# Scores on two halves of TensorE's rows, and units of the dilated attention taken two at a time

## The chip, the cores and the metric

One core of a Trainium2 chip runs the whole kernel. It has TensorE (matmuls, into PSUM), VectorE, ScalarE and GpSimd (called POOL in the profile), and SyncE, whose queue issues most of the transfers. The metric is the time of one execution on the device in microseconds; the median of several is given. Lower is better.

## The reference

The reference is a trunk of two layers on 512 tokens of width 1024, in float32. Each layer is a norm, a mixer, a residual, a norm, a gated feed-forward part with a short convolution, a residual. The mixer of layer 0 is a gated DeltaNet beside a dilated window attention (8 heads of 64); that of layer 1 is a retention (4 heads, keys of 64, values of 128) beside a Hyena convolution. The change touches the two parts that multiply q with k. The dilated attention is, cut to what matters:

```python
q, k = rope(q), rope(k)                      # 8 heads, 64 wide
for window, dilation in ((128, 1), (512, 4), (2048, 16)):
    s = where(valid, q @ k.T * 64 ** -0.5, -1e30)      # banded, per residue class of the dilation
    o_p, lse_p = softmax(s) @ v, logsumexp(s)
o = sum_p softmax_p(lse_p) * o_p
```

The retention is, for both directions together, `o = ((q @ k.T) * decay) @ v` per head, where decay depends on the distance of two tokens, followed by a norm and a gate; q and k are rotated here too.

## The kernel before

Everything is one program on one core, written with tiles; a planner orders the instructions of each engine, mostly in the order in which the program gives them, and takes a later one first where an earlier one is not ready by its own estimate of times. PSUM is two pools of four banks: `acc` and `wk`. A matrix product in float32 is done as three fp32r matmuls on a split of each operand into hi and lo (`mm3`, lines 263 to 265). Weights come by SyncE's queue in 512 KB pieces, and ScalarE and VectorE split them (lines 251 and 252).

The dilated attention (`dilated`) joins its three patterns into one softmax over all 512 keys, with the logarithm of the number of patterns that allow a distance added to the score (`lnc`). Two heads of 64 lie in one tile of 128 rows, a pair p. Its q and k come from a projection (`proj_t`), and are rotated: `rope_in` copies PSUM to SBUF and swaps halves by four DMAs; `rope_out` multiplies, adds, and makes the matmul operands. For q it makes for each head a tile of 128 rows that has hi in one half of the rows and lo in the other; for k (`moving`) one with hi in both halves, by a copy on POOL, and one with lo in one half and zeros in the other. So a score tile of a head, `mm_stack`, is two matmuls over 128 rows: (hi + lo) of q with hi of k, and hi of q with lo of k.

The work goes in 16 units (p, i): pair p, block i of 128 queries. `scores` makes for each of the two heads a 128 x 512 score tile in a `wk` bank; VectorE adds lnc, takes the extreme and writes smx (line 524), ScalarE takes the exponential with its sum (line 525), VectorE the reciprocal, POOL scales (line 529). `turn` transposes the two tiles on TensorE into `acc` banks (line 535), and ScalarE and VectorE copy one each into pT (line 537). `pv` multiplies with v: each matmul is 128 rows by 64 columns, the two heads of the pair on two halves of the columns (line 546). In the loop over u the scores are those of unit u, the transposes those of u - 2, the products those of u - 3; at u = 0, 2, 5 and 8 the projection of a later q or k stands behind them, at u = 10 and 18 a piece of the gates of the next part (`tail`).

The retention (`retention`) has two pairs s of two heads. For each head h, `scores(h)` makes four score tiles by `mm_stack` in `wk` banks, and VectorE multiplies each with the decay `gen` into sd (line 1079); the decays of all four heads are made ahead. Then 16 matmuls in plain float32 (two passes each) multiply with v (line 1089). The scores of head h + 1 are put ahead of the products of head h. Before this, `proj_tok` makes v: four pieces of weights, 24 matmuls for each, into four `acc` banks, which ScalarE copies out (line 1060).

Of the kernel before, what the change touches and what calls it, by code (L numbers as in the profile page):

```python
# [162 lines left out]
class K:  # L163
# [129 lines left out]
    def proj_tok(self, n, out_fn, filler=None):  # L293

        accs = [self.acc(nm=f"pt{t}") for t in range(NT)]
        for c in range(4):
            w = self.get()
# [163 lines left out]
    def rope_out(self, pool, rope, t, sw, moving, tag, bufs):  # L461


        nc = self.nc
        nc.gpsimd.tensor_mul(sw, sw, rope[:, 1, :])
        nc.vector.tensor_mul(t, t, rope[:, 0, :])
        nc.vector.tensor_add(t, t, sw)
        o = pool.tile([128, 4 if moving else 2, S], F32R, tag=tag, name=tag, bufs=bufs)
        half = [slice(0, 64), slice(64, 128)]
        for e in range(2):  # L470
            a, b = half[e], half[1 - e]
            nc.scalar.copy(o[a, e], t[a])
            nc.vector.tensor_sub(o[a, 2 + e] if moving else o[b, e], t[a], o[a, e])
            if moving:
                nc.gpsimd.memset(o[b, 2 + e].bitcast(F32), 0.0)
                nc.gpsimd.tensor_copy(o[b, e], o[a, e])
        return o
# [5 lines left out]
    def mm_stack(self, out, a, b, e, cols):  # L483
        self.nc.tensor.matmul(out, a[:, e, cols], b[:, e], start=True, stop=False)
        self.nc.tensor.matmul(out, a[:, e, cols], b[:, 2 + e], start=False, stop=True)
# [14 lines left out]
    def dilated(self, n, tail):  # L500
        nc, I = self.nc, self.I
        V = nc.vector
        with ExitStack() as ctx:
# [7 lines left out]
            def project(p, what, ps=None):  # L511
# [3 lines left out]
                qk[p, what] = self.rope_out(dp, rope, *self.rope_in(dp, ps)[:2], what == "k", "d" + what, 3)  # L515
# [40 lines left out]
            for i in range(4):  # L556
# [3 lines left out]
                if i < 2:  # L560
                    qk[0, "qk"[i]] = self.rope_out(dp, rope, *rin[i][:2], i == 1, "d" + "qk"[i], 3)
            with self.tc.issue_after(rin[3][2].ins):
                for i in (2, 3):
                    qk[1, "qk"[i % 2]] = self.rope_out(dp, rope, *rin[i][:2], i == 3, "d" + "qk"[i % 2], 3)
# [841 lines left out]
```

## Time and profile before

| | |
|---|---|
| median of 3 runs | 1319.92 us (1319.66 to 1320.06) |
| the profiled execution | 1319.69 us, of which the profile's span is 1317.9 us |
| TensorE busy | 1302.9 us, 6977 matmul records |
| VectorE, ScalarE, POOL busy | 750.7, 526.9, 144.4 us |
| dilated attention, scores to last product | from 61 to 135 us |
| retention, scores and products | from 748.7 to about 770 us |

How to read it: a matmul's recorded duration includes the time until its last result is written, so matmuls overlap in the record; what one costs TensorE is its pitch, from its start to the start of the next. "L484" is line 484. A float32 matmul that isn't fp32r is recorded as two passes. In a timeline, neighbours of one line are merged into one row with a count, from the first start to the last end.

### The profile page before, as it was taken

Reading aid. Unit: us, or ns where it says so; the run is one execution under the profiler, and the core shown is the slowest. Engines: PE = TensorE matmul, PEld = TensorE weight load, DVE = VectorE, ACT = ScalarE, POOL = GpSimd, SP = SyncE. Lnnn points to the kernel's source line nnn. Section 1 sums busy time; section 2 is a strip of 40 time slices with the busy share of each in tenths; the row PEclk is TensorE's granted clock in tenths of the full one; section 3 lists DMA queues with packets and bytes.
Section 4 is the critical chain, followed back from the end, with each engine's and each line's share of the span. In section 5 each row is a group of like instructions: output and inputs, shape, how many; then the busy total and the mean of one; then the engine's idle time right before and its main releaser. Section 6 shows DMA issues by size and latency. Waiting matters only on the chain.

```text
span 1317.9 us, 17629 instructions
## 1 busy us (share of the span) xinstructions
PE 1302.9 (99%) x6977; PEld 1092.6 (83%) x6977; DVE 750.7 (57%) x1089; ACT 526.9 (40%) x837; POOL 144.4 (11%) x175
## 2 busy tenths in 40 slices
PE   8999999999999999999999999999999999999997
PEld 7877888888988888888889887888888888888886
DVE  5777659977744432444437828879754443344432
ACT  5466548235433321333326334532433331133332
POOL 2454120013000000000002200024100000000001
PEclk9999999999999999999999999999999999999999
DMA  7430113411333332333323513330343333233321
GB/s 227 127 103 25 52 33 112 130 49 61 119 101 99 98 96 81 112 96 96 96 80 112 163 41 100 93 96 19 90 122 99 99 99 96 81 113 96 96 80 64
DMA packets 161025, 123.61 MB, mean 94 GB/s; under 512 B 6985, under 2 KB 134477, under 8 KB 160944
## 3 DMA queue, kind: packets, MB, share of 16 engines
q1 hardware_dynamic: 160798, 122.43, 31.6%
q8 instruction: 55, 0.90, 0.3%
q14 instruction: 26, 0.21, 0.1%
q10 hardware_dynamic: 146, 0.07, 0.0%
HBM read 117.23 MB, written 2.10 MB: 91 GB/s over the span
## 4 chain that ended last, share of the span: by engine, by line
PE 87%; DVE 7%; ACT 2%; DMA 1%; issue 1%; SPq 1%; POOL 1%; POOLq 0%; ACTq 0%; DVEq 0%
PE gup L264 11%; PE gup L265 11%; PE gup L263 11%; PE oacc L264 7%; PE oacc L265 7%; PE oacc L263 7%; PE pt L263 2%; PE pt L264 2%; PE pt L265 2%; PE first L264 2%; PE first L265 2%; PE first L263 2%; PE ap L263 1%; PE ap L264 1%; PE ap L265 1%; PE hap L263 1%
## 5 line engine op out<-in xcount | busy, mean ns | idle before, releaser
L252 DVE TENSOR_TENSOR wlo<-raw,whi 128x1024 fp32r<-128x1024 f32 x192 | 236.2, 1232 | 305.0 <-ACT whi L251 300.3
L251 ACT CAST whi<-raw 128x1024 fp32r<-128x1024 f32 (+1 forms) x197 | 206.1, 1047 | 424.7 <-PE gup L264 183.7
L263 PE MATMUL gup<-hh,whi 128*128 128x512 f32 x656 | 255.2, 389 | 0.0
L264 PE MATMUL gup<-hl,whi 128*128 128x512 f32 x656 | 255.2, 389 | 0.0
L265 PE MATMUL gup<-hh,wlo 128*128 128x512 f32 x656 | 255.2, 389 | 0.0
L263 PEld LDWEIGHTS gup<-hh,whi 128*128 128x128 f32 x656 | 123.2, 188 | 25.6
L264 PEld LDWEIGHTS gup<-hl,whi 128*128 128x128 f32 x656 | 123.2, 188 | 25.4
L265 PEld LDWEIGHTS gup<-hh,wlo 128*128 128x128 f32 x656 | 123.2, 188 | 25.4
L263 PE MATMUL oacc<-whi,ghi 128*128 128x512 f32 x352 | 137.1, 389 | 0.0
L265 PE MATMUL oacc<-whi,glo 128*128 128x512 f32 x352 | 137.0, 389 | 0.0
L264 PE MATMUL oacc<-wlo,ghi 128*128 128x512 f32 x352 | 136.9, 389 | 0.0
L265 PEld LDWEIGHTS oacc<-whi,glo 128*128 128x128 f32 x352 | 66.1, 188 | 13.7
L263 PEld LDWEIGHTS oacc<-whi,ghi 128*128 128x128 f32 x352 | 66.1, 188 | 13.7
L264 PEld LDWEIGHTS oacc<-wlo,ghi 128*128 128x128 f32 x352 | 66.1, 188 | 13.6
L428 DVE TENSOR_TENSOR sl<-gup,sl 128x512 f32<-128x512 f32 x42 | 29.0, 692 | 81.1 <-PE gup L265 81.1
L313 DVE TENSOR_TENSOR x<-oacc,x 128x512 f32<-128x512 f32 x64 | 43.2, 684 | 48.6 <-PE oacc L265 48.6
L427 ACT ACTIVATE sl<-c 128x512 f32<-128x512 f32 x44 | 27.8, 632 | 89.2 <-DVE c L365 89.2
L263 PE MATMUL first<-hh,whi 128*128 128x256 f32 x192 | 54.9, 288 | 0.0
L264 PE MATMUL first<-hl,whi 128*128 128x256 f32 x192 | 54.4, 284 | 0.2 <-DVE hl L224 0.2
L265 PE MATMUL first<-hh,wlo 128*128 128x256 f32 x192 | 54.2, 283 | 0.0
L104 POOL TENSOR_SCALAR ss<-ss 128x1 f32<-128x1 f32 x16 | 5.0, 311 | 429.3 <-ACT jk L102 429.3
L263 PE MATMUL pt<-whi,hh 128*128 128x512 f32 x128 | 50.1, 391 | 0.1
(422 smaller groups left out, 2336.4 us busy)
## 6 DMA issues: line engine op xcount, KB each, us to landing
raw<-in_ffn_w_in_dram SPq DMA_DIRECT2D x88, 512.0 KB, 3.8
raw<-in_ffn_w_out_dram SPq DMA_DIRECT2D x44, 512.0 KB, 3.7
raw<-in_ab_w_in_dram SPq DMA_DIRECT2D x28, 512.0 KB, 3.9
raw<-in_cd_w_in_dram SPq DMA_DIRECT2D x24, 512.0 KB, 4.6
x<-in_x_dram SPq DMA_DIRECT2D x16, 256.0 KB, 4.2
raw<-in_ab_w_out_dram SPq DMA_DIRECT2D x8, 512.0 KB
raw<-in_cd_w_out_dram SPq DMA_DIRECT2D x8, 512.0 KB, 3.6
rs<-rt SPq DMA_DIRECT2D x32, 64.0 KB, 2.0
```

Source lines behind the costliest of these rows:

```text
L104: nc.gpsimd.tensor_scalar(ss[:, 1:2], ss[:, 0:1], s, EPS, op0=ALU.add, op1=ALU.add)
L251: self.nc.scalar.copy(hi, raw)
L252: (self.nc.gpsimd if self.pool_lo else self.nc.vector).tensor_tensor(lo, raw, hi, op=ALU.subtract)
L263: mm(out, a[0], b[0], start=start, stop=False)
L264: mm(out, a[0], b[1], start=False, stop=False)
L265: return mm(out, a[1], b[0], start=False, stop=stop)
L313: self.nc.vector.tensor_add(xs, acc, xs)
L427: nc.scalar.activation(sl, c, AF.Silu)
L428: nc.vector.tensor_mul(sl, up, sl)
```

## The change

`mm_stack` is replaced by `mm_pair`: a matmul takes only the 64 rows of its head, three of them make a score tile (hi with hi, hi with lo, lo with hi), and those of the two heads of a pair alternate, the one on rows 0 to 63 and the other on rows 64 to 127, each into a bank of its own. So `rope_out` needs only hi and lo of the whole tile, by one copy on ScalarE and one subtraction on VectorE; the copies and fills on POOL go, and the tile is half as large for k. In the dilated part the loop takes two units at a time: scores of u and u + 1 (a projection directly behind the scores of its unit), transposes of u - 2, products of u - 4 and u - 3, transposes of u - 1; smx has eight buffers, not six. In the retention, `scores(s)` does both heads of a pair, with the decays of these two heads ahead of it; the first stands ahead of the last of the four pieces of v's projection (`RS` = 3), the second behind the products of the first head; sd has three buffers for each j, not two.

```diff
-    def proj_tok(self, n, out_fn, filler=None):
+    def proj_tok(self, n, out_fn, within={}):
 
         accs = [self.acc(nm=f"pt{t}") for t in range(NT)]
         for c in range(4):
+            within.get(c, lambda: None)()
...
-    def rope_out(self, pool, rope, t, sw, moving, tag, bufs):
-
+    def rope_out(self, pool, rope, t, sw, tag, bufs):
 
         nc = self.nc
         nc.gpsimd.tensor_mul(sw, sw, rope[:, 1, :])
         nc.vector.tensor_mul(t, t, rope[:, 0, :])
         nc.vector.tensor_add(t, t, sw)
-        o = pool.tile([128, 4 if moving else 2, S], F32R, tag=tag, name=tag, bufs=bufs)
-        half = [slice(0, 64), slice(64, 128)]
-        for e in range(2):
-            a, b = half[e], half[1 - e]
-            nc.scalar.copy(o[a, e], t[a])
-            nc.vector.tensor_sub(o[a, 2 + e] if moving else o[b, e], t[a], o[a, e])
-            if moving:
-                nc.gpsimd.memset(o[b, 2 + e].bitcast(F32), 0.0)
-                nc.gpsimd.tensor_copy(o[b, e], o[a, e])
+        o = pool.tile([128, 2, S], F32R, tag=tag, name=tag, bufs=bufs)
+        self.split(o[:, 0], o[:, 1], t)
         return o
 
     def rope_room(self):
 
         return self.xp.tile([128, 2, S], F32, tag="xn", name="room")
 
-    def mm_stack(self, out, a, b, e, cols):
-        self.nc.tensor.matmul(out, a[:, e, cols], b[:, e], start=True, stop=False)
-        self.nc.tensor.matmul(out, a[:, e, cols], b[:, 2 + e], start=False, stop=True)
+    def mm_pair(self, outs, a, b, cols):
+
+        for x, y in ((0, 0), (0, 1), (1, 0)):
+            for e in range(2):
+                r = slice(64 * e, 64 * e + 64)
+                self.nc.tensor.matmul(outs[e], a[r, x, cols], b[r, y], start=x + y == 0, stop=x == 1)
...
             def scores(p, i):
                 st = self.sm.tile([128, 6], F32, tag="st", name="st", bufs=8)
                 o = 384 - 128 * i
-                for e in range(2):
-                    sp = self.wk(nm="sp")
-                    self.mm_stack(sp, qk[p, "q"], qk[p, "k"], e, slice(i * 128, i * 128 + 128))
-                    s_ = dp.tile([128, S], F32, tag="smx", name="smx", bufs=6)
+                sps = [self.wk(nm="sp") for _ in range(2)]
+                self.mm_pair(sps, qk[p, "q"], qk[p, "k"], slice(i * 128, i * 128 + 128))
+                for e, sp in enumerate(sps):
+                    s_ = dp.tile([128, S], F32, tag="smx", name="smx", bufs=8)
...
-            for u in range(len(units) + 3):
-                if u < len(units):
-                    scores(*units[u])
-                if 0 <= u - 2 < len(units):
-                    turn(*units[u - 2])
-                if 0 <= u - 3:
-                    pv(*units[u - 3])
-                if later and u in DPROJ[:4]:
-                    project(*later.pop(0))
+            nu = len(units)
+            for u in range(0, nu + 4, 2):
+                for w in (u, u + 1):
+                    if w < nu:
+                        scores(*units[w])
+                    if later and w in DPROJ[:4]:
+                        project(*later.pop(0))
+                for w in (u - 2, u - 4, u - 3, u - 1):
+                    if w == u - 2 or w == u - 1:
+                        if 0 <= w < nu:
+                            turn(*units[w])
+                    elif 0 <= w:
+                        pv(*units[w])
                 if u in DPROJ[4:]:
...
-            self.proj_tok(n, lambda t, a: nc.scalar.copy(v[:, t, :], a))
...
-            def scores(h):
-                q, k = qk[0, h // 2], qk[1, h // 2]
+            def scores(s):
+                for h in (2 * s, 2 * s + 1):
+                    nc.scalar.activation(gen[:, h, :], rel[0], AF.Copy, scale=ld[:, h:h + 1])
+                    V.scalar_tensor_tensor(gen[:, h, :], rel[1], ld[:, 4 + h:5 + h], gen[:, h, :], op0=ALU.mult, op1=ALU.add)
+                    nc.scalar.activation(gen[:, h, :], gen[:, h, :], AF.Exp)
                 for j in range(4):
-                    sp = self.wk(nm="rsp")
-                    self.mm_stack(sp, k, q, h % 2, slice(j * 128, j * 128 + 128))
-                    t = rp.tile([128, S], F32, tag=f"sd{j}", name=f"sd{j}", bufs=2)
+                    sps = [self.wk(nm="rsp") for _ in range(2)]
+                    self.mm_pair(sps, qk[1, s], qk[0, s], slice(j * 128, j * 128 + 128))
                     o = 384 - 128 * j
-                    V.tensor_mul(t, sp, gen[:, h, o:o + 512])
-                    sd[h, j] = t
-
-            scores(0)
+                    for e, sp in enumerate(sps):
+                        h = 2 * s + e
+                        t = rp.tile([128, S], F32, tag=f"sd{j}", name=f"sd{j}", bufs=3)
+                        V.tensor_mul(t, sp, gen[:, h, o:o + 512])
+                        sd[h, j] = t
+
+            self.proj_tok(n, lambda t, a: nc.scalar.copy(v[:, t, :], a), {RS: lambda: scores(0)})
             O = [self.acc((128, 4, 128), f"ro{t}") for t in range(4)]
             for h in range(4):
-                if h < 3:
-                    scores(h + 1)
                 for i in range(4):
                     for j in range(4):
                         nc.tensor.matmul(O[i][:, h, :], sd[h, j][:, i * 128:(i + 1) * 128], v[:, j, h * 128:(h + 1) * 128], start=(j == 0), stop=(j == 3))
+                if h == 0:
+                    scores(1)
...
+RS = 3
```

## Rows read from the trace of the kernel before

**Rows 1.** The page: span, busy time of two engines, the chain by engine.

```profile
span 1317.9 us, 17629 instructions
...
PE 1302.9 (99%) x6977; PEld 1092.6 (83%) x6977; DVE 750.7 (57%) x1089; ACT 526.9 (40%) x837; POOL 144.4 (11%) x175
...
PE 87%; DVE 7%; ACT 2%; DMA 1%; issue 1%; SPq 1%; POOL 1%; POOLq 0%; ACTq 0%; DVEq 0%
```

**Rows 2.** Busy times by stretches: PE, PEld, DVE, ACT, POOL (instructions), clock, DMA.

```profile
91.00:105.00 14.00, 14.00 (x107) 11.42 (x107) 10.96 (x24) 9.27 (x20) 6.17 (x8) 1.00 0.22 57
115.00:130.00 15.00, 15.00 (x140) 12.30 (x140) 12.16 (x33) 10.46 (x26) 7.49 (x11) 1.00 0.01 2
```

**Rows 3.** Timeline of TensorE, one unit: start, length, line, tile, count.

```profile
93.97 0.50 PE L484 MATMUL sp<-dk,dq 128*128 128x512 f32 x1
94.31 0.40 PE L485 MATMUL sp<-dk,dq 128*128 128x512 f32 x1
...
95.02 1.03 PE L535 MATMUL tp<-ident,smx 128*128 128x128 f32 x8
95.98 1.09 PE L546 MATMUL op<-pT,dv 128*64 128x128 f32 x16
97.01 0.50 PE L484 MATMUL sp<-dk,dq 128*128 128x512 f32 x1
```

**Rows 4.** The same, cut where the shape changes (from 93.70 and from 95.75).

```profile
93.44 0.61 PE L546 MATMUL op<-pT,dv 128*64 128x128 f32 x8
...
95.56 0.49 PE L535 MATMUL tp<-ident,smx 128*128 128x128 f32 x3
```

**Rows 5.** All score matmuls of the dilated part: shortest, median, longest.

```profile
L484 PE MATMUL sp<-dk,dq x32: 387/397/504, 61.1 to 127.8; 128*128 128x512 f32 x32
...
L485 PE MATMUL sp<-dk,dq x32: 390/393/499, 61.3 to 128.0; 128*128 128x512 f32 x32
```

**Rows 6.** Timeline of TensorE, 64x64 transposes on two halves of the rows.

```profile
267.85 0.41 PE L917 MATMUL vp<-ident,P 64*64 64x64 f32 x4
...
269.35 0.63 PE L917 MATMUL vp<-ident,P 64*64 64x64 f32 x12 [0.20 <-DVE P L903]
```

**Rows 7.** All of these transposes: shortest, median, longest.

```profile
L917 PE MATMUL vp<-ident,P x32: 216/216/245, 267.8 to 272.0; 64*64 64x64 f32 x32
```

**Rows 8.** Evictions and exponentials of smx: shortest, median, longest.

```profile
L524 DVE CUSTOM_DVE_ANT_0 smx<-sp,lnc x32: 657/686/692, 61.7 to 129.3; 128x512 f32<-128x512 f32 x32
L525 ACT ACTIVATE smx<-smx,st x32: 706/722/728, 62.7 to 130.1; 128x512 f32<-128x512 f32 x32
```

**Rows 9.** Copies of the transposed tiles: shortest, median, longest.

```profile
L537 DVE COPY pT<-tp x16: 670/685/692, 72.0 to 133.4; 128x512 f32<-128x512 f32 x16
L537 ACT COPY pT<-tp x16: 562/586/587, 72.0 to 133.1; 128x512 f32<-128x512 f32 x16
```

**Rows 10.** Timeline of TensorE, the one wait of the stage, in brackets.

```profile
81.11 0.63 PE L535 MATMUL tp<-ident,smx 128*128 128x128 f32 x4 [0.70 <-ACT pT L537]
```

**Rows 11.** Groups by line, 0 to 250 us: copies and subtractions of rope_out.

```profile
L476 POOL CAST dk<-dk 64x512 fp32r<-64x512 f32 x8 | 7.1, 892 | 8.0 <-ACT dk L472 7.7
...
L473 DVE TENSOR_TENSOR dq<-rt,dq 64x512 fp32r<-64x512 f32 x8 | 5.5, 686 | 1.6 <-ACT dq L472 1.4
```

**Rows 12.** Timeline of TensorE, scores of the retention's first two heads.

```profile
748.70 0.39 PE L484 MATMUL rsp<-r,r 128*128 128x512 f32 x1
...
751.88 0.38 PE L1089 MATMUL ro<-rv,sd 128*128 128x128 f32 x2
...
752.56 0.38 PE L1089 MATMUL ro<-rv,sd 128*128 128x128 f32 x2
```

**Rows 13.** Timelines of VectorE and of ScalarE, the same place.

```profile
749.35 4.87 DVE L1079 TENSOR_TENSOR sd<-rsp,gen 128x512 f32<-128x512 f32 x8 [2.22 <-PE rsp L485]
...
748.90 0.59 ACT L1060 COPY rv<-pt 128x512 f32<-128x512 f32 x1 [0.77 <-PE pt L265]
```

More of the change, by code (lines that the diff above doesn't have):

```diff
@@ L514, in project @@
                     self.proj_t(self.get(), n, ps)
-                qk[p, what] = self.rope_out(dp, rope, *self.rope_in(dp, ps)[:2], what == "k", "d" + what, 3)
+                qk[p, what] = self.rope_out(dp, rope, *self.rope_in(dp, ps)[:2], "d" + what, 3)
             def scores(p, i):
@@ L560, in dilated @@
                 if i < 2:
-                    qk[0, "qk"[i]] = self.rope_out(dp, rope, *rin[i][:2], i == 1, "d" + "qk"[i], 3)
+                    qk[0, "qk"[i]] = self.rope_out(dp, rope, *rin[i][:2], "d" + "qk"[i], 3)
             with self.tc.issue_after(rin[3][2].ins):
                 for i in (2, 3):
-                    qk[1, "qk"[i % 2]] = self.rope_out(dp, rope, *rin[i][:2], i == 3, "d" + "qk"[i % 2], 3)
+                    qk[1, "qk"[i % 2]] = self.rope_out(dp, rope, *rin[i][:2], "d" + "qk"[i % 2], 3)
             self.proj_tok(n, lambda t, a: nc.scalar.copy(v[:, t, :], a))
@@ L1046, in rot @@
                 which, s = i // 2, i % 2
-                qk[which, s] = self.rope_out(rp, rope, *rin[i][:2], which == 0, f"r{which}{s}", 1)
+                qk[which, s] = self.rope_out(rp, rope, *rin[i][:2], f"r{which}{s}", 1)
             for i in range(4):
@@ L1065, in retention @@
             nc.sync.dma_start(ld, bc(I["ret_log_decay"].rearrange("o d h -> o (d h)"), [128, 8]))
-            for h in range(4):
-                nc.scalar.activation(gen[:, h, :], rel[0], AF.Copy, scale=ld[:, h:h + 1])
-                V.scalar_tensor_tensor(gen[:, h, :], rel[1], ld[:, 4 + h:5 + h], gen[:, h, :], op0=ALU.mult, op1=ALU.add)
-                nc.scalar.activation(gen[:, h, :], gen[:, h, :], AF.Exp)
             sd = {}
-            def scores(h):
-                q, k = qk[0, h // 2], qk[1, h // 2]
+            def scores(s):
[3 more added lines that the diff above has]
+                    nc.scalar.activation(gen[:, h, :], gen[:, h, :], AF.Exp)
                 for j in range(4):
-                    sp = self.wk(nm="rsp")
-                    self.mm_stack(sp, k, q, h % 2, slice(j * 128, j * 128 + 128))
-                    t = rp.tile([128, S], F32, tag=f"sd{j}", name=f"sd{j}", bufs=2)
+                    sps = [self.wk(nm="rsp") for _ in range(2)]
+                    self.mm_pair(sps, qk[1, s], qk[0, s], slice(j * 128, j * 128 + 128))
                     o = 384 - 128 * j
-                    V.tensor_mul(t, sp, gen[:, h, o:o + 512])
-                    sd[h, j] = t
-            scores(0)
+                    for e, sp in enumerate(sps):
[4 more added lines that the diff above has]
+            self.proj_tok(n, lambda t, a: nc.scalar.copy(v[:, t, :], a), {RS: lambda: scores(0)})
             O = [self.acc((128, 4, 128), f"ro{t}") for t in range(4)]
             for h in range(4):
-                if h < 3:
-                    scores(h + 1)
                 for i in range(4):
@@ L1089, in retention @@
                         nc.tensor.matmul(O[i][:, h, :], sd[h, j][:, i * 128:(i + 1) * 128], v[:, j, h * 128:(h + 1) * 128], start=(j == 0), stop=(j == 3))
+                if h == 0:
+                    scores(1)
             Os = []
             for t in range(4):
-                o = rp.tile([128, 4, 128], F32, tag=f"sd{t}", name=f"ros{t}", bufs=2)
+                o = rp.tile([128, 4, 128], F32, tag=f"sd{t}", name=f"ros{t}", bufs=3)
                 (V.tensor_copy if t % 2 else nc.scalar.copy)(o, O[t])
```

## The prediction

> **What bounds the kernel now.** I read the page first: the busy times, then the chain that ended last. TensorE is busy for 1302.9 of 1317.9 us and carries 87% of the chain; VectorE, the next, is busy 57% of the time [rows 1]. So the time is a sum of TensorE's pitches, and another engine counts only where TensorE stands and waits for it. Then the table by stretches, for the stage that the change rewrites, the dilated attention (about 61 to 135 us): from 91 to 105 and from 115 to 130 us TensorE is busy throughout, and VectorE has 12.16 of 15 us there, ScalarE 10.46 [rows 2]. There is some slack on them, but not much. Then TensorE's own timeline, one unit of that stage [rows 3], and cuts of it at the places where the shape of the tile changes [rows 4]. The reader is to see two things in these. A unit starts its scores at 93.97 and the next at 97.01, so it takes 3.04 us: 1.05 for four score matmuls, 0.96 for eight transposes, 1.03 for the sixteen passes of the product with v. And the change of tile shape costs time each way. The last transpose starts at 95.56 + 2 x 0.108 = 95.78, the first 128x64 matmul 0.20 later, of which 0.108 is the transpose itself: about 0.09 us in which nothing streams. Going back, the first score matmul is recorded with 0.50 us, not 0.40, and the second starts 0.34 behind it where the others follow in 0.235: the weight load, otherwise hidden, is in the open with 0.107 us.
>
> **Scores on two halves of the rows.** Before, a score tile is two matmuls over all 128 rows, with hi and lo stacked: two lines with 32 each in the dilated part [rows 5], so 64, and by the code 4 heads x 4 tiles x 2 = 32 in the retention. After, it is three matmuls of 64 rows; two heads' matmuls alternate on the two halves. If the halves run side by side, a pair of heads costs three pitches where it cost four. No row shows a 512-column matmul on a half. The nearest shows 64x64 tiles of which the two kinds start on rows 0 and 64 and write the same columns: four of them alone take 0.41 us, twelve take 0.63 [rows 6], where one lasts 0.216 [rows 7]. The pitch from the first is (0.41 - 0.216) / 3 = 0.065, so twelve in a row would take 0.216 + 11 x 0.065 = 0.93; eight starts give 0.67. So eight of the twelve ran as four pairs. The bounds of a pair are thus one pitch (0.235 us) and two (0.47); I take one, since that is what the nearest row shows.
>
> The Trainium skill ("TensorE: Matmul & The Clock Gate", section Measured speedup vs the span model) gives 3.07 times for four row tiles of 512 columns, not 4. If halves lost as much, an estimate from that page, a pair would take 0.235 x 4 / 3.07 = 0.31 us; the rows here show no such loss, but on shorter matmuls. It is rival four below.
>
> **Two units at a time.** The cost of a switch decides what is left of that. Before, each unit makes one round trip, transposes to 128x64 and back to scores; the scores and the transposes have one shape. After, the scores have a shape of their own. A step of two units is: scores of both, transposes, two products with v, transposes. Its four stretches, each with its own drain of 0.09 and its open first load (0.107, or half of that, an estimate, for the transposes' and the 64-column loads):
> scores 6 x 0.235 + 0.107 + 0.09 = 1.61; transposes 0.96 + 0.05 = 1.01, twice; products 1.03 + 8 x 0.11 = 1.91 (the pair pitch from (0.61 - 0.273) / 3 in [rows 4]). Sum 5.54, where two units took 6.08. Eight steps: 44.3 for 48.6 us. Three of the four projections stand between the scores of one step; by the order of the loop there are ten visits to the half-row shape, not eight, at 2 x (0.09 + 0.107) = 0.4 each: +0.8. Before, the last two units shared one trip: 0.35 less on its side. Together 45.1 for 48.25: the dilated part gains **3.2 us** on TensorE. Nothing covers TensorE there, so this comes off the end, if no new wait arises.
>
> Waits: the transposed tiles have four pT buffers; the copies of one unit now wait until the product two units back has read its own, and behind them on ScalarE and VectorE stand exponentials and the next evictions. By the durations in a step of 5.5 us, VectorE has four evictions of 0.69 [rows 8] and two copies of 0.68 [rows 9], 4.1 us, ScalarE four exponentials of 0.72 and two copies of 0.57, 4.0 us; the second transposes of a step come when the copies are just done. So I cost this at nothing, and up to 0.2 us a step, 1.6 in all, if ScalarE is late. The wait of before that ends at 81.11, where TensorE stood 0.70 us for such a copy near a projection [rows 10], can go or stay; I leave it in. The four smx buffers of a step are covered by the eight.
>
> **rope_out.** The eight POOL copies of 0.89, the fills beside them, and half of the half-tile subtractions (0.69 each; one for a whole tile is of that length) go [rows 11], in the dilated part and likewise in the retention. They lie beside TensorE's projections; nothing late depends on them in the rows of the stage, so they are worth nothing, and relieve POOL and VectorE. The DMAs of the swap (rs) stay as they are.
>
> **Retention.** The matmuls there go from 32 pitches to 24, 5.5 us for 7.3. But eight score tiles come in a row, through four PSUM buffers, and VectorE empties one in 4.87 / 8 = 0.61 us [rows 13]. Before, TensorE made one in 0.455 and the eight just fitted: only the last was held back, by one product, at 751.88 [rows 12]. After, it makes one in 0.34. I work it out with no other work between: the first is done at 2 x 0.227 + 0.39 = 0.85, VectorE releases the four buffers at 1.6, 2.2, 2.8 and 3.4; the third pair of tiles can run side by side only from 2.2, the last from 3.4, and ends at 4.13. With 0.4 for the trip to the other shape that is 4.53, against (752.56 - 748.70 - 0.21) = 3.65 for eight before: **+0.9 us** for each of the two groups. Moved ahead of the last quarter of v's projection, the first group no longer covers the copy of v's last tile, which ScalarE starts at 748.90 and ends at 749.49, about 0.2 after the first three products could have run [rows 13]: **+0.2**. So the retention loses **2.0 us**. The bounds: if other matmuls fill the waits and pairs stay pairs, two trips and no wait, 2.73 + 0.8 = 3.5 a group, nothing lost; if buffers come free one by one and heads run alone, 1.4 + 2.7 + 0.8 = 4.9 a group, 2.7 lost in all. The value taken is near the middle; VectorE also has weight splits to do in that stretch, which makes the lower bound less likely.
>
> **Sum.** -3.2 + 2.0 = -1.2 us. The profiled execution took 1319.69 us, 1.8 more than its span; 1318.5 after. The median of the runs is 0.23 higher, so 1319.92 - 1.2 = **1318.7 us**.
>
> **The rivals.**
> One: the queue fills the waits of the retention (products and v's projection between the pairs), and the wait before 81.11 goes with the changed order. Then -3.2 - 0.7 + 0 = -3.9: 1316.0 us. For it: there is other work at both places, and the order before did put a product between two score matmuls [rows 12]. Against it: each such filling is another trip of 0.4.
> Two: the copies of the transposed tiles come late in each step (four pT and four accumulator buffers for more tiles in flight), 0.2 to 0.4 us in eight steps, and the retention's heads run alone: -3.2 + 2.4 + 2.7 = +1.9, 1321.8 us. For it: the wait before 81.11 is of that kind. Against: all the other units of before show none.
> Three, the slower one: halves of 512 columns do not run side by side. A pair then costs 0.47. In the dilated part 48 pairs x 0.235 = +11.3, in the retention a group takes 12 x 0.45 + 0.4 = 5.85, not 4.53: +2.6. Together +12.7: 1332.6 us. It decides from the point where a pair takes 0.235 + (1.2 + 2.64) / 48 = 0.315 us. Against it stand [rows 6]; for it, that these rows are short tiles whose matmuls take in half a column a cycle, so the array's outputs may not have been loaded as two full streams would.
> Four: the halves run side by side, but with a loss, so that a pair takes some 0.31 us: 48 x 0.075 = +3.6 on the forecast, 1322.3 us.
> That the change does not do what it says would be three: matmuls that are issued as pairs and run one behind the other.
>
> **How the numbers follow.** Forecast (within 1317.3 to 1320.2) 0.47, rival one 0.30, two 0.10, three 0.07, four 0.06. About 0.2%, 2.64 us, is what a measurement of this kernel can tell from no change. Faster by that: rival one but for its weakest fifth, plus a tenth of the forecast's share whose retention loses little: 0.24 + 0.10 = 0.34. Slower: rival three, most of four and a little of two: 0.13. The rest, 0.53, is within 0.2%. The range of 8 in 10 reaches to rival one's best side, 1319.92 - 4.4 = 1315.5, and to rivals two and four, 1322.3; outside lie three, and the ends of one and four.
>
> **What would show each step.** In the trace after: score matmuls in pairs a few ns apart, a pair every 0.23 us (three and four fall) or not. A step of two units, from scores to scores, of 5.5 us where no projection stands in it (if 5.9 or more, look for a wait of a transpose for pT: two). Score stretches of the dilated part ten in number. In the retention, TensorE waiting for VectorE's sd in the middle of each group, about 1.4 us in each, or other matmuls standing there (one). The forecast is wrong if the order of the queue splits the pairs in the dilated part, which I have taken to hold since the four buffers are free again long before the next step.

## The result and the profile after

The changed kernel takes 1328.12 us (median; 1326.91 to 1330.41), beside 1319.79 us (1319.50 to 1320.06) for the kernel before in the same comparison: a ratio of 1.0064, 95% interval 1.0054 to 1.0075. It is 8.3 us slower. Forecast were 1318.7 us and a range of 1315.5 to 1322.3 us, so the time lies above the range, on the other side of no change. The profiled execution after took 1329.21 us, 1.8 more than its span, as before; it is 9.5 us longer than the one of before.

The page after, the lines that answer to [rows 1]:

```profile
span 1327.4 us, 17668 instructions
...
PE 1306.0 (98%) x7025; PEld 1089.4 (82%) x7025; DVE 737.9 (56%) x1077; ACT 519.5 (39%) x825; POOL 129.1 (10%) x151
...
PE 85%; DVE 7%; ACT 3%; issue 2%; DMA 2%; POOL 1%; SPq 1%; POOLq 0%; ACTq 0%; DVEq 0%
```

The span is 9.5 us longer and TensorE is busy 3.1 us more. So two thirds of the loss are TensorE standing still: 15.0 us of the span before, 21.4 after. VectorE, ScalarE and POOL all have less to do than before, and that has not helped.

Where the time went is read from the starts of TensorE's tiles: the same tile's first matmul in both timelines, and the differences of those starts. The dilated part (from the first score matmul `sp` to the transposes of `rowp` behind it) took 74.54 us and takes 77.37: +2.83. From there to the retention's `rqk`: +0.81. From `rqk` to the first `hap` of the Hyena stage: +2.97. From there to the end: +2.63. The forecast for these four was -3.2, 0, +2.0 and 0.

**The dilated part.** TensorE's timeline (start, length, line, tile and shape, count, in brackets the idle time before it and what ended it): the three larger waits of the part, then one step of two units without a projection:

```profile
78.96 0.63 PE L531 MATMUL tp<-ident,smx 128*128 128x128 f32 x4 [1.43 <-ACT rt L457]
...
97.61 0.63 PE L531 MATMUL tp<-ident,smx 128*128 128x128 f32 x4 [1.42 <-ACT pT L533]
...
116.45 0.63 PE L531 MATMUL tp<-ident,smx 128*128 128x128 f32 x4 [0.99 <-POOL smx L525]
...
120.69 1.67 PE L481 MATMUL sp<-dk,dq 64*128 64x512 f32 x12
122.29 1.09 PE L531 MATMUL tp<-ident,smx 128*128 128x128 f32 x8
123.32 1.97 PE L542 MATMUL op<-pT,dv 128*64 128x128 f32 x32
125.21 0.66 PE L531 MATMUL tp<-ident,smx 128*128 128x128 f32 x4
126.04 0.63 PE L531 MATMUL tp<-ident,smx 128*128 128x128 f32 x4 [0.17 <-ACT pT L533]
126.60 1.65 PE L481 MATMUL sp<-dk,dq 64*128 64x512 f32 x12
```

The four stretches of a step come out at what the prediction had: scores 122.29 - 120.69 = 1.60 us (1.61), transposes 1.03 (1.01), products 125.21 - 123.32 = 1.89 (1.91). The second transposes take 126.60 - 125.21 = 1.39, 0.36 more, since their second half waits. Before had one wait of this kind [rows 10]; now five of the eight steps have one at their second transposes, and three of them cost over 1 us each.

What the second of these waits waited for is seen on the other engines (their timelines, same stretch; SPq is SyncE's queue of DMA issues):

```profile
88.79 2.41 SPq L459 DMA_DIRECT2D rs<-rt  x4
...
93.82 1.78 POOL L465 TENSOR_TENSOR rs<-rs,rope 128x512 f32<-128x512 f32 x1 [3.76 <-DMA rs<-rt]
...
93.78 0.69 DVE L466 TENSOR_TENSOR rt<-rt,rope 128x512 f32<-128x512 f32 x1 [0.44 <-DMA rs<-rt]
...
95.64 0.69 DVE L467 TENSOR_TENSOR rt<-rt,rs 128x512 f32<-128x512 f32 x1 [0.56 <-POOL rs L465]
...
96.36 0.62 ACT L223 CAST dq<-rt 128x512 fp32r<-128x512 f32 x1 [0.37 <-DVE rt L467]
96.89 0.58 ACT L533 COPY pT<-tp 128x512 f32<-128x512 f32 x1
```

Read it as a chain. A projected tile's swap is issued from 88.79 in four DMAs. When they have landed, POOL multiplies for 1.78 us, VectorE stands 0.56 us for POOL before it adds (95.64), ScalarE stands 0.37 us for VectorE before it takes the hi part (96.36), and only behind that, at 96.89, comes the copy that frees the accumulator bank for which TensorE has been standing since 96.19 (97.61 less 1.42). From 95.99 ScalarE stands idle although that copy could run: its tile is transposed by 93.70, and the products that free its buffer end at 95.60. So ScalarE takes its instructions here in the order they are queued in, and the rotation of a tile that is done at 98.5 and needed only at 120.69, by the scores of the last pair, stands ahead of a copy that is needed at once. The waits at 78.96 and 116.45 have the same rotation (of the tiles `dq` and `dk`) ahead of them.

A rotation also fills its step. Busy times (columns as in [rows 2]) of the step with the second wait, of the one without a projection, and of a step of run E7 below:

```profile
91.03:98.17 7.14, 5.72 (x62) 4.47 (x62) 5.84 (x14) 4.46 (x12) 3.15 (x3) 1.00 0.36 94
120.69:126.60 5.91, 5.75 (x62) 4.48 (x61) 4.14 (x12) 3.99 (x10) 2.12 (x4) 1.00 0.01 3
...
89.99:95.51 5.52, 5.52 (x61) 4.50 (x61) 5.42 (x14) 3.68 (x10) 1.91 (x2) 1.00 0.49 128
```

Without a rotation VectorE works 4.14 us in a step, with one 5.84, more than the 5.5 us that a whole step was to take. But the last row, E7's, has a rotation as well, 5.42 us of VectorE's work in 5.52, and TensorE does not stand in it at all. So the work just fits, where the rotation stands behind the copies.

**The retention.** Timelines of ScalarE and TensorE at its start, then TensorE and VectorE at the scores:

```profile
712.81 1.98 ACT L1069 ACTIVATE gen<-rel,ld 128x896 f32<-128x896 f32 x2 [2.65 <-DMA ld<-in_ret_log_decay_dram]
714.70 1.05 ACT L223 CAST hh<-nt 128x512 fp32r<-128x512 f32 x2
...
716.76 0.38 PE L264 MATMUL first<-hl,whi 128*128 128x256 f32 x1 [0.68 <-DVE hl L224]
...
747.26 1.66 PE L481 MATMUL rsp<-r,r 64*128 64x512 f32 x12
...
748.49 1.23 DVE L252 TENSOR_TENSOR wlo<-raw,whi 128x1024 fp32r<-128x1024 f32 x1 [3.15 <-ACT whi L251]
749.63 4.87 DVE L1079 TENSOR_TENSOR sd<-rsp,gen 128x512 f32<-128x512 f32 x8
...
750.37 2.76 PE L481 MATMUL rsp<-r,r 64*128 64x512 f32 x12 [0.79 <-DVE sd L1079]
...
761.94 4.51 PE L481 MATMUL rsp<-r,r 64*128 64x512 f32 x24
```

At the start, the decays (`gen`) are now queued on ScalarE ahead of the split of the normed tile (`hh`) and wait 2.65 us for the load of `ld`; the split comes behind them and TensorE's first projections wait for its second half. Before, ScalarE did the split first. At the scores, the second group goes in one visit, from 761.94 to the next product at 766.38: 4.44 us, where 4.53 was forecast. The first group is cut: after twelve matmuls two of v's projection stand between, and then TensorE waits, since VectorE does a weight split (`wlo`, 1.23 us) before its first eviction.

**Hyena.** SyncE's queue, TensorE's timeline, and the busy times of the stretch behind it (columns as in [rows 2]; the granted clock is the third number from the end):

```profile
803.40 1.44 SPq L1144 DMA_DIRECT2D bf<-in_hy_f_dram  x1
...
811.84 1.04 PE L1148 MATMUL hm<-mlp,w 33*64 33x512 f32 x2 [1.25 <-DMA w<-in_hy_w_dram]
```

```profile
813.00:817.00 4.00, 4.00 (x11) 3.11 (x11) 2.76 (x5) 0.93 (x1) 0.00 (x0) 0.57 0.29 74
```

Nothing was changed there. One of four small DMA issues takes 1.44 us, where it took 0.60 before, the weight load queued behind it comes later, and the matmul that needs it waits 1.25 us, where it waited 0.18. Right behind that the granted clock is 0.57 in the mean of 4 us, so for most of it TensorE runs at the lower of its two levels, 1.2 GHz: there are 11 matmuls in 4 us, where the same stretch holds 18 at full clock (run E5 below).

### The profile page after: what moved, and what is told of

Its sections match the earlier page's. It is cut to its first block, busy times and chain, and to the rows that moved or that the text cites. A ratio compares the mean times of both kernels' runs of the same rounds, so it can differ in the third digit from the quotient of the medians.

```text
span 1327.4 us, 17668 instructions
## 1 busy us (share of the span) xinstructions
PE 1306.0 (98%) x7025; PEld 1089.4 (82%) x7025; DVE 737.9 (56%) x1077; ACT 519.5 (39%) x825; POOL 129.1 (10%) x151
## 4 chain that ended last, share of the span: by engine, by line
PE 85%; DVE 7%; ACT 3%; issue 2%; DMA 2%; POOL 1%; SPq 1%; POOLq 0%; ACTq 0%; DVEq 0%
PE gup L263 11%; PE gup L264 11%; PE gup L265 11%; PE oacc L265 7%; PE oacc L264 7%; PE oacc L263 7%; PE first L264 2%; PE pt L265 2%; PE pt L263 2%; PE first L263 2%; PE pt L264 2%; PE first L265 2%; PE ap L264 1%; PE ap L263 1%; PE ap L265 1%
## 5 line engine op out<-in xcount | busy, mean ns | idle before, releaser
L265 PE MATMUL pt<-whi,hl 128*128 128x512 f32 x128 | 50.0, 390 | 0.0
```

What stands on the lines that cost most here:

```text
L265: return mm(out, a[1], b[0], start=False, stop=stop)
```

## The experiments

Each run has the kernel before beside it on the same chip; a ratio is to that. Where a part's change is given, it is the difference of starts of the same tiles against the profile of before, as above; "dilated", "start", "retention" and "Hyena" are the four stretches named there. Ahead of them the profiled executions differ by up to 1.1 us (the first score matmul starts at 61.05 us in before, and at 61.99 in E12, whose code there is that of before), so a stretch says more than the whole of one profile.

**E1 and E2: one half of the change alone.** E1 has the dilated attention of after and the retention of before, E2 the reverse; each holds the code of both ways of scoring.

```
 retention (E1)                       dilated (E2)
-  mm_pair(sps, qk[1, s], qk[0, s], ..)   -  mm_pair(sps, qk[p,"q"], qk[p,"k"], ..)
+  mm_stack(sp, k, q, h % 2, ..)          +  mm_stack(sp, qk[p,"q"], qk[p,"k"], e, ..)
   and rope_out, the decays, the order of the loop, as before
```

> The dilated attention is that of after (scores on two halves, two units at a time), the retention that of before (two matmuls over 128 rows for a score tile, and its own stacked operands). Theory: the two traces show the dilated part 2.9 us longer (first score to the end of the products 77.0 us for 74.2), from three waits of a second transpose of 1.2 to 1.6 us each; nothing else of the change is in this kernel, so 1319.8 + 2.9 = 1322.7 us, and the wait for w3 and the half clock in the Hyena part (2.7 us in the trace of after) are gone, since they come from the retention's changed end. Rival: the Hyena part's loss comes from what is fetched and issued after the changed dilated part, whatever the retention does: 1319.8 + 2.9 + 2.7 = 1325.4 us.

> The retention is that of after, the dilated attention that of before (with its stacked operands). Theory: in the traces the retention's start loses 0.9 us (the split of the last transposed tile stands behind the decays on ScalarE, which waits for a small transfer), its scores and products 3.0, the Hyena part 2.7: 1319.8 + 6.6 = 1326.4 us, with about 1.5 us of spread from the last term. Rival: the last term belongs to the dilated part's change: 1323.7 us. The two halves of the change are additive in either case: the gains of this kernel and of the dilated one alone should sum to 8.3 us.

E1: 1323.80 us, ratio 1.0031 (1.0019 to 1.0043); dilated +2.83, retention 0.0, Hyena +0.81. E2: 1323.93 us, ratio 1.0033 (1.0022 to 1.0045); dilated 0.0, start +0.88, retention +2.89, Hyena -0.2. The two losses, 4.0 and 4.15 us, add up to 8.2 of the 8.3 us of the whole, and the waits of each part stand in its own run: neither part brings the other's about. In E1 Hyena loses, in E2 not, although neither kernel touches it; so the theories of both runs on that loss were wrong.

**E3: eight pT buffers.**

```
-  t = dp.tile([128, 4, 128], F32, tag="pT", name="pT", bufs=4)
+  t = dp.tile([128, 4, 128], F32, tag="pT", name="pT", bufs=8)
```

> After, with eight pT buffers in the dilated part, not four, and nothing else. Theory: the second transposes of a step wait because the copy of the first cannot be written before the product two units back has read its own pT, and then stands on ScalarE behind the rotation of a projected tile; with eight buffers the copies are put ahead of it, the waits of 1.6, 1.6 and 1.2 us go, and 1328.1 - 4 = 1324 us. Rival: the copies stand behind the rotation's cast on ScalarE (which waits for VectorE and POOL) whatever buffers there are: no change, 1328 us.

1325.59 us, ratio 1.0047 (1.0030 to 1.0063); dilated +0.93, that is 1.9 us better than after. The wait that stood at 97.61 is gone, the first is not:

```profile
79.35 0.63 PE L531 MATMUL tp<-ident,smx 128*128 128x128 f32 x4 [1.34 <-ACT rt L457]
```

The third of the large waits is there too, now at `bap` (1.24 us). More buffers let the copies of a step wait for less, but ScalarE's `rt` (L457) that this row names is itself an instruction of the rotation: it empties a projection's accumulator, and stands in line behind the rotation of the tile before.

**E4: one unit at a time**, in the loop's order of before, everything else of after.

```
-  for u in range(0, nu + 4, 2): ...
+  for u in range(len(units) + 3):
+      scores(u); turn(u - 2); pv(u - 3); project
```

> After, with the dilated loop of before: one unit at a time (scores of u, transposes of u - 2, products of u - 3, projection), scores on two halves of the rows as in after. Theory (waits): the waits go with the two units at a time. By the pitches a unit takes 3 x 0.235 + 0.107 + 0.09 for scores, 1.01 for transposes, 1.03 for products, 2.94 us where before took 3.04; so the dilated part gains 1.3 us on before, and the whole is 1328.1 - 2.9 - 1.3 = 1323.9 us. Rival (switches): each change of tile shape costs more than the 0.2 us that I took; then this kernel, with 16 visits to the half-row shape where after has 11, is slower than after: 1330 us or more.

1325.88 us, ratio 1.0050 (1.0035 to 1.0065); dilated +1.60. An undisturbed unit:

```profile
95.25 0.96 PE L481 MATMUL sp<-dk,dq 64*128 64x512 f32 x6
96.14 1.09 PE L531 MATMUL tp<-ident,smx 128*128 128x128 f32 x8
97.16 1.09 PE L542 MATMUL op<-pT,dv 128*64 128x128 f32 x16
98.19 0.97 PE L481 MATMUL sp<-dk,dq 64*128 64x512 f32 x6
```

It takes 98.19 - 95.25 = 2.94 us, where before took 3.04 [rows 3], the size that the pitches and switches of the prediction give: scores 0.89, transposes 1.02, products 1.03. So these terms are right, in either order of the loop, and the waits are another matter: here they stand at the products.

**E5 and E6: the four small loads early**, E5 on after, E6 on before.

```
 load_ffn_consts / first loads of the program
+  self.hy_bf = self.cst.tile([64, 4], F32, name="bf")
+  for i, nm in enumerate(("hy_b1", "hy_f1", "hy_b2", "hy_f2")):
+      nc.sync.dma_start(self.hy_bf[:, i:i + 1], I[nm]...)
 hyena_filters
-  bf = hp.tile([64, 4], F32, name="bf")   (and its four loads)
+  bf = self.hy_bf
```

> The changed kernel with the four small loads of the Hyena filters' biases (bf) issued among the first loads of the program, and not in the stage. Theory: the loss at the head of the Hyena stage (TensorE waits 1.25 us for a weight load of that stage, then part of the next stretch is at half clock) comes from SyncE's queue, where the four issues, one of 1.44 us, stand ahead of the loads waited for; gone with them, 2 us or so (1.0 to 2.7): 1326.1 us. Rival: the load waited for is late by itself, whatever stands ahead of it: not over 0.4 us is gained, 1327.8 us.

> The same move of the four small loads in the kernel before, where the same matmul waits 0.18 us. Theory: 0 to 0.3 us are gained, 1319.6 us. Rival: the issues cost as much there, 1 us or more, 1318.5 us or less.

E5: 1326.54 us, ratio 1.0052 (1.0037 to 1.0067); Hyena -0.17, where after had +2.63, and the clock stays up:

```profile
811.13 1.07 PE L1149 MATMUL hm<-mlp,w 33*64 33x512 f32 x2
```

```profile
812.00:816.00 4.00, 4.00 (x18) 3.20 (x18) 3.48 (x6) 1.72 (x2) 0.00 (x0) 1.00 0.41 137
```

E6: 1319.60 us, ratio 0.9998 (0.9989 to 1.0007): the same move is worth nothing where no issue is slow. So the loss at Hyena comes through those issues. Over all the profiles the two go together: the slow issue takes 1.05 us in E1, 1.29 in E3, 1.14 in E4, 1.04 in E7, 1.12 in E8, 1.59 in E13, and the matmul then waits 1.00, 0.78, 0.63, 0.72, 0.59 and 0.95 us; in before, E2 and E12 no issue is over 0.60, and the waits are 0.18, none and 0.37. What makes the issue slow is not settled, but one thing always goes with it. In after, a packet of the instruction queue lies in that moment (transfers between 803.2 and 805.2 us), in before none does:

```profile
q8 instruction: 1, 0.02, 3.0%
```

It is so in all ten profiles that have these loads in the stage. In the seven with a slow issue a packet of 16 KB of that queue runs into this issue, which ends 0.37 to 0.41 us after the packet; in before, E2 and E12 the packet comes 7.1 to 7.2 us behind the last of the four issues. That fits a fetch of program code for which the issue waits, and a program whose code lies elsewhere would then meet it elsewhere; no run moved the code alone.

**E7 and E13: the rotation a step later.** A projection's `rope_in` stays where it is, its `rope_out` is put behind the copies of the next step's second transposes; `rs` gets a second buffer. E7 has seven pT buffers, E13 the four of after.

```
 project(p, what)
-  qk[p, what] = self.rope_out(dp, rope, *self.rope_in(dp, ps)[:2], "d" + what, 3)
+  pend.append((p, what, self.rope_in(dp, ps)[:2]))
 end of the next step
+  with self.tc.issue_after(last copy of pT):
+      qk[p, what] = self.rope_out(dp, rope, *r, "d" + what, 3)
```

> The changed kernel with the rotation of each later projection put behind the second transposed tiles' copies of the next step (its swap loads have one step more to land), and seven pT buffers for four. Theory: the waits of the dilated part are VectorE and ScalarE standing at the rotation for POOL and the swap, with copies and exponentials behind them; without them the part takes about 71.5 us, where the changed kernel takes 77.0: 1328.1 - 5.5 = 1322.6 us. Rival: the copies are late since four of them and four evictions come in a row, whatever the rotation does; then only the buffers tell, as in the run with eight of them, 1325.6 us.

> The changed kernel with the rotation of the later projections put behind the transposed tiles' copies of the next step, and its four pT buffers left as they are. The fourth corner beside the changed kernel, the run with eight pT buffers and the run with both. Theory: the place of the rotation is the larger part; the dilated part's loss against before (2.8 us) turns into a gain of 1 us or more, 1328.1 - 4 = 1324.1 us, and a copy that waits for a pT buffer costs a few tenths in some steps. Rival: with four buffers the copies stand whatever the rotation does, and the buffers are what turned the loss into a gain: 1327 us.

E7: 1322.40 us, ratio 1.0018 (1.0009 to 1.0028), where after has 1.0064; dilated -2.13. E13: 1323.57 us, ratio 1.0026 (1.0016 to 1.0037); dilated -1.13. With E3 that makes a square, in us against before:

| dilated part | rotation as in the change | rotation a step later |
|---|---|---|
| pT: four buffers | +2.83 (after) | -1.13 (E13) |
| pT: seven or eight | +0.93 (E3) | -2.13 (E7) |

The place of the rotation is worth 4.0 and 3.1 us, the buffers 1.9 and 1.0. The second `rs` buffer goes with the place, and no run has it alone; in after the one buffer had been read (until 77.66) before the next swap was issued (78.84), so it does not explain the first wait. In E7, VectorE's and TensorE's timelines at the first rotation and at the second transposes of the step that had the wait of 1.42:

```profile
80.75 0.66 DVE L466 TENSOR_TENSOR rt<-rt,rope 128x512 f32<-128x512 f32 x1
...
81.95 0.68 DVE L467 TENSOR_TENSOR rt<-rt,rs 128x512 f32<-128x512 f32 x1
...
94.49 1.09 PE L535 MATMUL tp<-ident,smx 128*128 128x128 f32 x8
95.51 0.96 PE L481 MATMUL sp<-dk,dq 64*128 64x512 f32 x6
```

VectorE's two instructions have no bracket any more, and the transposes run as one eight. What is left in E7 are three waits of about 0.2 us (0.3 from start to start) in the steps behind the last projection. In E13 one more is seen, at 95.02, and the scores are once cut:

```profile
95.02 0.63 PE L535 MATMUL tp<-ident,smx 128*128 128x128 f32 x4 [0.30 <-POOL smx L529]
```

**E8: the retention in four visits.** The decays are put behind the copy of the second projected tile, the first group's scores stand ahead of the third and the fourth quarter of v's projection, the second's behind the products of head 0 and in the middle of those of head 1.

```
-  self.proj_tok(n, .., {RS: lambda: scores(0)})        # and scores(1) after head 0
+  with self.tc.issue_after(rin[1][2].ins): gens(0); gens(1)
+  self.proj_tok(n, .., {2: lambda: scores(0, (0, 1)), 3: lambda: scores(0, (2, 3))})
   head h, products of tile i:
+  if (h, i) in ((0, 3), (1, 1)): scores(1, (2 * h, 2 * h + 1))
```

> The changed kernel with the retention's scores in four visits of two tile pairs (the first group's ahead of the third and the fourth quarter of v's projection, the second's behind the products of head 0 and in the middle of those of head 1), and all decays behind the copy of the second projected tile, not ahead of a split of the normed tile. Theory: the start gets its 0.9 us back; a visit of 12 matmuls costs 1.70 us with its switches, four cost 6.8, where the two groups took some 5.45 + 4.5 = 9.95 with VectorE's evictions to wait for: 3.1 more. 1328.1 - 4.0 = 1324.1 us. Rival: the evictions and trips fill what the waits leave, and only the start is gained: 1327.2 us.

1324.48 us, ratio 1.0036 (1.0023 to 1.0049); start -0.19, where after had +0.81; retention +0.87, where after had +2.97. The two visits of the second group:

```profile
760.48 1.66 PE L481 MATMUL rsp<-r,r 64*128 64x512 f32 x12
762.07 2.05 PE L1092 MATMUL ro<-rv,sd 128*128 128x128 f32 x16
764.05 1.67 PE L481 MATMUL rsp<-r,r 64*128 64x512 f32 x12
765.65 2.61 PE L1092 MATMUL ro<-rv,sd 128*128 128x128 f32 x21
```

Two visits of 1.59 and 1.60 us take the place of one of 4.44. So the loss there was VectorE's pace over eight tiles in a row, and the start was the place of the decays. Even so the retention stays 0.87 us behind before. The second visit of the first group is still long, 2.52 us from its start to the next matmul's at 751.19, since VectorE gets to the tiles of the first visit only at 747.76, behind a weight split:

```profile
748.66 2.59 PE L481 MATMUL rsp<-r,r 64*128 64x512 f32 x12
```

That is 0.93 us more than the other three take. Without it, an estimate, the retention would stand where before does: four trips eat what the eight pitches less bring.

**E9 to E12: what the parts are worth.** E10 joins the dilated attention of E7, the retention of before and the loads of E5. E9 is E10 with the later projections behind units 1, 3, 5 and 7. E11 is E10 with one unit at a time. E12 is the kernel before with the rotation put two units later and nothing else.

```
 E9   -DPROJ = (0, 2, 5, 8, 10, 18)   +DPROJ = (1, 3, 5, 7, 10, 18)
 E11  the loop of E4                  E12  pend and issue_after as in E7, on before
```

> The retention of the kernel before, the small bf loads early, the dilated attention two units at a time with the rotation a step later and seven pT buffers, and the four later projections behind the odd units 1, 3, 5, 7 (not 0, 2, 5, 8), so that none stands between the scores of one step: eight visits to the half-row shape for ten. Theory: the stage gains 2.2 us against before, as in the run with the rotation later, and two trips of 0.4 us more: 1319.8 - 2.2 - 0.8 = 1316.8 us. Rival: a projection behind both units brings back waits of the transposes: 1318 us or more.

> The same with the projections where the change has them (units 0, 2, 5, 8). Theory: the parts add up; the stage 2.2 us shorter than before, nothing lost in the retention and at Hyena: 1319.8 - 2.2 = 1317.6 us. Rival: a loss of 0.5 to 2 us moves to another stage, as at Hyena's start before: 1318.5 us.

> The same as that, but one unit at a time, in the loop's order of before. Theory: a unit takes 2.94 us for 3.04, so 16 give 1.6 less than before, and with the rotation later no big wait is left; the visits split by a projection cost 0.4 each: 1319.8 - 1.2 = 1318.6 us, 1 us more than two units at a time. Rival: two at a time only adds tiles in flight; one at a time is as fast, 1317.6 us.

> The kernel before with nothing but the rotation of the later projections put two units later. Theory: its one wait of that kind (0.70 us, and 0.25 in others) goes at most: 1319.8 - 0.7 = 1319.1 us. Rival: the later rotation by itself brings what the runs with halves gained by it (some 3 us): 1316.8 us, and the halves have no part in it.

E10: 1318.47 us, ratio 0.9988 (0.9979 to 0.9997), the one version found that is faster than the kernel before, by 0.12%, and its interval only just leaves out a ratio of 1; dilated -2.15. It came in 0.9 us above what was expected. In its profile 0.8 us is given back at the end of the retention, where TensorE, which comes 1.2 us earlier than before, stands for VectorE:

```profile
792.33 1.38 PE L1053 MATMUL tp<-ident,ros 128*128 128x128 f32 x5 [0.39 <-DVE ros L1047]
```

E9: 1319.05 us, ratio 0.9993 (0.9985 to 1.0002); dilated -0.94 for the -3.0 expected. Its visits to the half-row shape are eight instead of ten, but a projection behind each of four steps in a row brings its rotation back into the queue beside copies, and the rival had it:

```profile
111.45 0.63 PE L560 MATMUL tp<-ident,smx 128*128 128x128 f32 x4 [0.43 <-ACT pT L562]
113.32 0.42 PE L646 MATMUL bap<-hh,wba 128*32 128x512 f32 x1 [1.24 <-DVE pT L562]
```

E11: 1321.14 us, ratio 1.0007 (0.9998 to 1.0016); dilated +0.87, against both theories. Here the first rotation came right behind the first unit's copies, not a step later, and VectorE stood at it as in after; the products wait for it:

```profile
77.69 0.69 DVE L470 TENSOR_TENSOR rt<-rt,rs 128x512 f32<-128x512 f32 x1 [2.52 <-POOL rs L468]
...
83.12 1.09 PE L571 MATMUL op<-pT,dv 128*64 128x128 f32 x14 [1.03 <-DVE pT L562]
```

From start to start that wait costs 2.48 - 1.02 = 1.46 us. Without it one unit at a time would be 0.6 us better than before, and two at a time are 2.15 better; by this reckoning, which no run shows without the wait, the larger part of the gain is the order by two.

E12: 1319.80 us, ratio 0.9999 (0.9990 to 1.0008); dilated 0.0. The wait of [rows 10] is still there, and as in E11 VectorE stands for POOL at the first rotation (1.86 us at 77.28):

```profile
82.06 0.63 PE L539 MATMUL tp<-ident,smx 128*128 128x128 f32 x4 [0.76 <-ACT pT L541]
```

So the edit did not do there what it was made for, and the run doesn't settle what a later first rotation is worth to the kernel before. The rival falls: the order of the rotation of the other tiles brings before nothing, so the 2.15 us of E10 are not that edit's alone.

## Why the prediction was wrong

**The step that failed: the waits of the dilated part,** and with it the sentence on `rope_out` that "nothing late depends on them". The prediction summed durations per step (VectorE 4.1, ScalarE 4.0 of 5.5 us) and found slack, so it put the waits at nothing and up to 1.6 us in all. That slack is there in a step without a rotation (VectorE 4.14 us); the sum left the rotation out, with which VectorE has 5.84 us. And what slack there is, is of no use where an in-order engine stands at an instruction whose input is late: E7 has a rotation in a step of 5.52 us and no wait. Two things were in rows and not followed up. [rows 10] names the wait of before and the prediction says it stands near a projection, but not what ScalarE had done until then. And the rotation was costed by what the change removes from it, not by where it stands in the queues that the change tightens. Rival two had the kind of wait right (a late copy) and its price too low: it gave 0.2 to 0.4 us a step, 2.4 in all, but the waits cost 5.1 more than before's, most of it in three of 1.2 to 1.6 us each, in steps where a tile is rotated. Its cause, too few buffers, is the smaller part (1.9 us in E3).

**The sum of the dilated part, term by term.** The time from the first start of a run of one tile's matmuls to the first start of the next run, summed over the part by tile, in us:

| tile | before | after | E7 |
|---|---|---|---|
| scores sp | 16.73 | 14.20 | 13.31 |
| projections dqk | 22.16 | 22.53 | 22.57 |
| transposes tp | 15.33 | 21.24 | 17.11 |
| products op | 16.24 | 15.19 | 15.19 |
| bap | 3.71 | 3.85 | 3.88 |
| sum | 74.17 | 77.01 | 72.06 |

The scores and the products gained 2.5 and 1.05 us, and the transposes lost 5.9: about 5.2 are waits, the rest the switches that now stand on both sides of them. Taking its 1.16 us of waits out, E7's scores, transposes and products are 44.45 us, to which come 0.41 and 0.17 that projections and `bap` lose as neighbours of another shape: 45.0, where the prediction had 45.1. Before, taking out its 0.95, they are 47.35, where the prediction had 48.25: sixteen units at 3.04 each are too many, since a unit beside a projection or `bap` has no open weight load there (the shape is the same). So the gain without waits is 2.3 us, not **3.2**; this term was mis-sized by 0.9. Three further score visits came where two were counted: in after the queue put one score matmul between two halves of the transposes at 109.1 us.

**Halves side by side: right.** Twelve matmuls in 1.59 us, less the 0.197 of the switches, are 0.232 us a pair; forecast was 0.235. In the trace of after the two matmuls of an undisturbed pair start 1 to 6 ns apart, and the pairs of the dilated part follow each other in 0.231 us. Rivals three and four fall. The section Measured speedup vs the span model of the Trainium skill's page "TensorE: Matmul & The Clock Gate", by which the prediction made rival four (an estimate of 0.31 us a pair), gives its loss for four row tiles; with two, on these rows, there is none.

**The cost of a switch: right,** 0.09 us drained and 0.107 in the open, in E4 and in every undisturbed step.

**The retention: +2.0 forecast, +2.97 measured, and +0.81 not forecast.** The group in one visit was right (4.44 for 4.53). The other was mis-sized by 0.8 us (747.26 to 753.06, less the two matmuls between: 5.35 for 4.53): the bound for a group that the queue cuts was in the prediction, but the weight split on VectorE ahead of the evictions was only mentioned, at no price. The products took 0.5 us more as well, 14.46 for 13.95 by the same sums; of the 0.2 us forecast for the copy of v's last tile some 0.05 shows, one pitch of 0.158 us for 0.112. The start was not looked at at all: the change moves the loads of `rel` and `ld` and the decays, and where these then stand in ScalarE's queue was not followed. E8 gives the start back, and of the rest all but 0.87.

**Hyena: +2.63, not forecast,** and nothing in the text of the change points to it; of it 1.25 - 0.18 = 1.07 us are the wait, and (18 - 11) x 0.227 = 1.6 us the lower clock behind it. E5 shows the way that it takes.

**The sum, mended:** -2.3 without waits, +5.1 of waits (6.1 in after, the score visit cut at 109.1 among them, 0.95 in before), +0.8, +3.0 and +2.6 make +9.2, of the 9.5 us between the two profiled executions; the remaining 0.3 lies ahead of the dilated part and in the roundings of the parts.

## What to carry to other kernels

Before an order is tightened, follow each multi-engine chain in it (here projection, swap by DMA, POOL, VectorE, ScalarE) from its first to its last link, and look which instructions stand behind each link in the in-order queues: here the late link, and not the busy shares, set what came out. A chain whose result is needed much later belongs behind the work that is needed now. And cost a repeated unit from the sum over the stage, not from one undisturbed unit times their number.

## What the runs showed of the hardware

Two heads' 64-row matmuls of 512 columns in fp32r, one on each half of the array's rows, run fully side by side: 0.232 us a pair, where one over 128 rows has a pitch of 0.235 (three in 0.71 us from 94.31 on, [rows 3]).

A wait of TensorE can cost more than itself. After the wait at Hyena in after, the granted clock was 0.57 in the mean of 813 to 817 us; in E13 it was 0.68 in 748 to 752 us, behind the wait of the retention's scores:

```profile
748.00:752.00 4.00, 4.00 (x14) 2.87 (x14) 3.02 (x6) 0.27 (x1) 0.00 (x0) 0.68 0.34 102
```

Matmuls have a pitch of 0.43 us there for 0.227, and E13's retention is 1.5 us longer than after's for it. In the other profiles waits of 0.6 to 1.0 us at the same places left the clock at 1.00, so the same wait does not always cost it. It may be part of the wider spread of after (3.5 us between its executions, 0.6 for before); no run shows that.

A DMA issue on SyncE is not a constant: the same four small loads take 0.59 or 0.60 us each in before, and one of them 1.04 to 1.59 in kernels that differ from it elsewhere, each time beside a 16 KB packet of the instruction queue.
